# Moving 96 + 336 + 468 float32r matmuls to a fixed distance of 192 bytes between their two operands, and four small accumulations from ScalarE to VectorE

## The chip, the core and the metric

The kernel runs on one core of a Trainium2 chip. The metric is device time in microseconds; each number is the median of several runs of the whole program. A core has TensorE for matrix products (the profile's PE, with the weight loads shown beside it as PEld), VectorE (DVE), ScalarE (ACT), GpSimd (POOL, used here to issue DMAs) and SyncE (SP, which issues most loads). On-chip memory has 128 partitions, and a tile occupies the same bytes of each. "Distance" below always means the start address of a matmul's moving operand minus that of its stationary operand within a partition, modulo 256 bytes.

## What is computed

Two layers over 512 tokens of width 1024, with 256 context tokens that only the first layer needs:

```python
for i in range(DEPTH):                      # DEPTH = 2
    shift, scale, gate = split(silu(c) @ ada_w[i] + ada_b[i], 3)
    hx = rmsnorm(x, norm_g[i]) * (1 + scale) + shift          # hc: the same for the context
    if i == 0: out = retention_mixer(hx, hc, ...)             # 4 heads, both directions
    if i == 1: out = gmlp_chunk_mixer(hx, ...)                # v, u, z projections, spatial mix, output
    x = x + gate * out
return rmsnorm(x, final_g)
```

Retention projects q, k, v, z for each head, scores the 512 latent tokens against 768 keys with a decay, multiplies with v, normalises, gates with silu(z) and projects out. The gMLP projects v (2048 wide), normalises it over its width, mixes it over 128 tokens, multiplies with u and silu(z), and projects back to 1024.

## The kernel before, in words

All large products run in float32r with both operands split into a high and a low part; `mm3` (line of `mm3` in the listing) issues three matmuls for one product of two 128-row blocks: low x high, high x low, high x high. Each matmul record in the profile has one weight load (LDWEIGHTS) before it. A product of two 2x2-block matrices is done with seven block products (B11, T1, T2, B21, T3, B22, T4) by the class `Product`; one block product is 24 matmuls with 256 moving columns: 4 blocks of the contraction, 2 output halves, 3 matmuls.

Three functions carry these products. In `features` and `outward` the activations (tiles `A[...]`, in slots `oA11` to `oS4`, and `hc`) are moving and the weights stationary. In `tokens` it is the other way round. The weights come by DMA into raw slots (`w0` to `w7`, `g0`, ...), and `Stream.upto` splits them two products ahead into one of four `hl` slots, ScalarE making the high part and VectorE the low one. `hl_tile(moves)` starts the tile 128 bytes later in the slot or not, by whether the weights move. `place_at` instead puts the first four weight tiles of the gMLP's v projection straight into `oS1`, `oS2`, `oA22`, `oS3` (tile name `hl_e`).

The stages in order of time: the first projection with the start of the context (to 56 us); eleven more quads of weights, the projections of all heads (to 327); `attend_two`, heads 0 and 1 (to 380); `out_two`, their output projection (to 419); `attend_one` and `project_out` for heads 2 and 3 (to 522); the v projection of the gMLP (to 600); then eight units u0 to u7 of its u and z projection. After u3 comes `out_pair` (685 to 725), the first quarter products of the output projection, with `y` tiles split by `halved_y` into two separate slots each and weights (`o2`) moving. After u6 and after u7 follows `out1`, the rest of the output projection: weights (`o`) moving, 512 columns wide, `y` tiles stationary in `hc` (`ya`), in two `g` slots (`yb`) and in `oA11` (`yc`). In `attend`, `v` moves 512 wide and the score tiles `ph`, `pl` (slots `t2`) are stationary, 12 such matmuls a step, 288 in all; `out1` has 180 of them.

Each unit uses one tile `vt` (slot `w7`), loaded by `load_vt` on SP's queue and scaled by `norm_vt` with four ScalarE instructions; `spatial` multiplies it during B22. Before `out_pair`, `w7` is also lent to the raw loads of `o2` (`Q.free.append("w7")`), and `load_vt(4)` follows in the text after `out_pair`. The instructions of SP need not be in the order of the text: the framework places them.

`between_modes` is a small plain float32 matmul of `ones` (two records in the trace) that the text puts between groups of products at chosen places.

Slots are laid out by `lay` in the order of its lists, so addresses follow from sizes (each rounded up to 32 bytes). Modulo 256, counted from `oA11`:

| slots | before | after |
|---|---|---|
| activations in `oA*`, `oS*`; `hc`, `s1`, `w4`, `w5`, `g3` | 0 | 0 |
| `s0`, `s2`, `s3`, `rope`, `w6`, `g2`, `w0`-`w3`, `w7`, `g0`, `g1` | 64 | 64 |
| `t2` (score tiles `ph`, `pl`) | 192 | 64 |
| weights in `hl`, stationary / moving | 64 / 192 | 64 / 192 |
| weights in `hl` for `o` (512 wide in `out1`) | 64 | 192, or 0 for j = 9, 11 |
| weights in `hl` for `o2` (`out_pair`) | 192 | 0 |
| weights in `oS1`, `oS2`, `oA22`, `oS3` (`hl_e`) | 0 | 192 |

and so, moving minus stationary:

| matmuls | before | after |
|---|---|---|
| activations with `hl` weights in either role, score products of `qk` (about 5,500, 256 wide) | 192 | 192 |
| `hl_e` weights with `oA11`, `oA12` (96, 256 wide) | 0 | 192 |
| `o2` weights with `y` in `out_pair` (336, 256 wide) | 128 (272), 192 (64) | 192 |
| `v` with `ph`, `pl` (288, 512 wide) | 64 | 192 |
| `o` weights with `ya`, `yb`, `yc` in `out1` (180, 512 wide or split in two at the end) | 64, or 0 for half of `yb` | 192 |

Of the kernel before, what the change touches and what calls it, by code (L numbers as in the profile page):

```python
# [8 lines left out]
F32R = mybir.dt.float32r  # L9
# [58 lines left out]
def hybrid_kernel(ctx, tc, xT_d, cT_d, cv_d, sv_d, rows_d, ada0_d, adag_d, w_d, rope_d, dec_d, ws_d, id_d, out_d):  # L68
# [14 lines left out]
        return sb.tile(shape, dt, tag=tag, name=name or tag, bufs=bufs)  # L83

    T2 = 11
    HL = 4

    def lay(sizes, bufs=1):  # L90
        for tag, n in sizes.items():
            st([P, n // 4], tag, name="lay", bufs=bufs)

    lay({"ones": 512, "sv": 448, "ident": 512, "eps": 4, "cpad": 1024, "root": 4, "lg": 32, "gs0": 64, "sh0": 64,
         "sq0": 16, "sq1": 16, "sq2": 16, "rs0": 1024, "rs1": 1024, "rs2": 1024, "shb": 16, "gate0": 32, "gs1": 32,
         "sh1": 32, "shs": 16, "la": 32, "lb": 32, "lc": 32, "sum0": 16, "sum1": 16, "bns": 256, "mv": 32, "rv": 16})
# [58 lines left out]
    class Stream:  # L155
# [54 lines left out]
        def upto(self, n, late=None):  # L210

            while self.done < min(n, self.limit or len(self.items)):
                q, name, uses, at, place = self.items[self.done]
                self.pump()
                r = self.raws[q, at]
                self.sum(self.done)
                if self.by_queue(q, name):
                    if (q, name) not in self.added:
                        self.add((q, name))
                    assert (q, name) in self.added  # L220
                hl = place() if place else hl_tile(q[0] in ("vz", "v", "z", "v1", "o2"))
# [141 lines left out]
    for i in range(UZ):  # L363
        Q.quad(("u", i), SINGLE)
        for u in RAWS:
            Q.load((("u", i), u), W, 3, parts_of(("u", i), u))
        if i == 3:
            for name in PAIRED:
                for q in OUT1:
                    Q.item(q, name)  # L370
            for u in ("11", "21", "12", "22"):
                for q in OUT1:
                    Q.load((q, u), W + ["w7"], 3, parts_of(q, u))
        if i == UZ - 2:
            add_out(2, range(2))
    add_out(2, (2, 3))
# [3 lines left out]
    A = {}  # L380

    def op(key):
        A[key] = st([P, 2, 4, HS], "o" + key, F32R)

    def keep(key, src, ks=(0, 4)):
        k = slice(*ks)
# [375 lines left out]
    def come(*what, then=None):  # L762


        made = []
        for kb, th in what:
            g, k = divmod(kb, 4)
            r = th // 2
            if r:
                f, h, l = cq[g][:, k, :], hc[:, 0, kb, :], hc[:, 1, kb, :]  # L770
            else:
                name = NAMES[th][g]
                if k == 0:
                    A[name] = st([P, 2, 4, HS], AT_S3.get(name, "o" + name), F32R)
# [387 lines left out]
    def v_tile(h, tag):  # L1162

        if h != 1:
            return st([P, 2, 2, 512], tag, F32R, name="v")
        i = hls[0] % HL
        hls[0] += 1
        o = 16 if i % 2 else 48
        t = st([P, 2048 + o], f"hl{i}", F32R, name="v")
        return t[:, o:].rearrange("p (a b n) -> p a b n", a=2, b=2)  # L1170

    def load_v(h):
        v = []
# [169 lines left out]

    def attend_one(h, qs, vs, wo, steps, own=()):

        og = [st([P, 2, 4, HS], tag, F32R, name="og") for tag in ("oS3", "oS4")]

        def turn(h, hf, flipped):
            for fp, src in enumerate(flipped):
# [10 lines left out]
    def attend_two(qs, vs, ds, q2):  # L1360
# [2 lines left out]
        at = {}  # L1363

        def operand(key):
            t = A[key] = st([P, 2, 4, HS], ROOM[key], F32R)
            return t

        def plain(key, tag):
# [364 lines left out]
    def y_sums():  # L1734
        v = st([P, 4, HS], "g0", name="yv")
        dve.tensor_tensor(v, y22, y21, ALU.subtract)
        halved_y("S1", v, "g2", "g3")
        yield
        dve.tensor_tensor(v, v, y11, ALU.add)
        yield  # L1740
# [3 lines left out]
        dve.scalar_tensor_tensor(l, v, -1.0, f32(h), ALU.mult, ALU.subtract)  # L1744
        yield
        dve.tensor_tensor(y12, v, y12, ALU.subtract)
        halved_y("S4", y12, "g2", "g3")
        yield
        dve.tensor_tensor(y21, y11, y21, ALU.subtract)
        halved_y("S3", y21, "g0", "g1")  # L1750
        yield
        halved_y("A22", y22, "g2", "g3")
        yield

    def out_pair():
# [3 lines left out]
        for name in PAIRED:  # L1759
            for q in OUT1:  # L1760
# [137 lines left out]
    for i in range(UZ):  # L1898
        got, pms = {}, {}
        prod = Product(features, got.__setitem__)  # L1900
        for name in SINGLE:
# [11 lines left out]
            if name == "B22":  # L1913
# [135 lines left out]
```

## Time and profile before

| | |
|---|---|
| median of 3 runs | 863.49 us (861.56 to 864.96) |
| the profiled execution | 861.68 us, with a span of 859.8 us from first to last instruction |
| granted TensorE clock, mean | 0.998 |
| TensorE matmul / weight load busy | 850.1 / 821.2 us |
| VectorE / ScalarE / GpSimd busy | 723.8 / 487.8 / 88.9 us |
| TensorE waiting by name | 1.1 us at the start, 0.9 us for a `pl` tile, 0.8 us for `ident` |

Matmul records overlap, because their ends include the way through the array. What one matmul costs is therefore read from starts: in the timeline, the start of a row, subtracted from the start of the next row, divided by the row's count, is the spacing of those matmuls.

### The profile page before, as it was taken

How to read it: one execution, taken by the hardware profiler on the slowest of the kernel's cores; microseconds unless marked ns; L12 is line 12 of the kernel's file. 1: busy time of each engine (PE TensorE's matmuls, PEld its weight loads, DVE VectorE, ACT ScalarE, POOL GpSimd, SP SyncE). 2: the span in 40 equal slices, each digit the busy share in tenths (PEclk: the TensorE clock that was granted, in tenths of full speed). 3: DMA queues.
4: the chain of work that ended last, by engine and by line, in shares of the span. 5: the costliest groups of instructions: out<-in, count | busy, mean ns of one | idle time of the engine just before them, and what ended most of it. 6: DMA issues, size and time to landing. Idle time of an engine off the chain costs nothing.

```text
span 859.8 us, 17428 instructions
## 1 busy us (share of the span) xinstructions
PE 850.1 (99%) x6966; PEld 821.2 (96%) x6966; DVE 723.8 (84%) x1015; ACT 487.8 (57%) x770; POOL 88.9 (10%) x132
## 2 busy tenths in 40 slices
PE   9999999999999999999999999999999999999996
PEld 7899999999999999899989899999999999999985
DVE  4799899869977985799687879998888998788895
ACT  4566644455365355567873559754656665565434
POOL 0001211211211011000001012121000010000110
PEclk9999999999999999999999999999999999999999
DMA  9945857876977797257486943547555557546532
GB/s 358 406 131 154 245 175 255 261 216 183 311 218 226 221 305 264 75 123 219 162 273 186 261 113 111 197 135 244 173 148 144 152 129 215 154 141 197 123 49 99
DMA packets 82049, 166.70 MB, mean 194 GB/s; under 512 B 8624, under 2 KB 39728, under 8 KB 81968
## 3 DMA queue, kind: packets, MB, share of 16 engines
q1 hardware_dynamic: 68592, 122.90, 43.4%
q0 software_dynamic: 12944, 42.48, 20.1%
q8 instruction: 55, 0.90, 0.4%
q10 hardware_dynamic: 432, 0.20, 0.1%
q14 instruction: 26, 0.21, 0.1%
HBM read 125.17 MB, written 24.12 MB: 174 GB/s over the span
## 4 chain that ended last, share of the span: by engine, by line
PE 94%; ACT 3%; DMA 1%; DVE 1%; issue 1%; ACTq 0%; DVEq 0%
PE pst L54 94%; DMA vt<-vt 1%; DMA ident<-in_id_dram 1%; ACT acc L54 0%; DVE o L54 0%; ACT L54 0%; ACT junk L54 0%; ACT hl L54 0%; ACT dt L54 0%; ACT vt L54 0%; ACT qk L54 0%; DVE snap L54 0%; ACT de L54 0%; DVE ada_h L54 0%; DVE v L54 0%
## 5 line engine op out<-in xcount | busy, mean ns | idle before, releaser
L54 DVE TENSOR_TENSOR hl<-raw,hl 128x1024 fp32r<-128x1024 f32 (+2 forms) x209 | 249.7, 1200 | 56.4 <-ACT hl L54 55.9
L54 ACT CAST hl<-raw 128x1024 fp32r<-128x1024 f32 (+2 forms) x209 | 214.4, 1031 | 128.6 <-DVE raw L54 61.9
L54 PE MATMUL pst<-oS,hl 128*128 128x256 f32 x1296 | 155.2, 277 | 0.1
L54 PEld LDWEIGHTS pst<-oS,hl 128*128 128x128 f32 x1296 | 150.6, 188 | 1.2 <-issue 0.8
L54 PE MATMUL pst<-hl,oS 128*128 128x256 f32 x1152 | 134.7, 276 | 0.0
L54 PE MATMUL pst<-oA,hl 128*128 128x256 f32 x1080 | 133.9, 279 | 0.1
L54 PEld LDWEIGHTS pst<-hl,oS 128*128 128x128 f32 x1152 | 132.4, 188 | 0.8 <-issue 0.4
L54 PEld LDWEIGHTS pst<-oA,hl 128*128 128x128 f32 x1080 | 127.3, 188 | 1.8 <-issue 0.4
L54 DVE TENSOR_TENSOR raw<-raw 128x1024 f32<-128x1024 f32 x77 | 93.9, 1220 | 0.9
L54 PE MATMUL pst<-hl,oA 128*128 128x256 f32 x768 | 92.1, 277 | 0.0
L54 ACT ACTIVATE snap<-pst 128x512 f32<-128x512 f32 x87 | 51.7, 594 | 68.0 <-PE pst L54 67.9
L54 PEld LDWEIGHTS pst<-hl,oA 128*128 128x128 f32 x768 | 89.3, 188 | 0.0
L54 PE MATMUL pst<-v,ph 128*128 128x512 f32 x192 | 59.8, 393 | 0.0
L187 POOL DMA_DIRECT2D raw<-raw x31 | 27.0, 870 | 278.8 <-DVE raw L54 166.9
L54 DVE TENSOR_TENSOR snap<-snap,pst 128x512 f32<-128x512 f32 x75 | 51.0, 680 | 3.0 <-PE pst L54 2.9
L54 PE MATMUL pst<-og,hl 128*128 128x256 f32 x384 | 46.3, 280 | 0.0
L54 PEld LDWEIGHTS pst<-og,hl 128*128 128x128 f32 x384 | 45.0, 188 | 0.2
L54 PEld LDWEIGHTS pst<-v,ph 128*128 128x128 f32 x192 | 36.1, 188 | 7.0
L54 PE MATMUL pst<-hl,ye 128*128 128x256 f32 x336 | 40.4, 282 | 0.0
L54 PEld LDWEIGHTS pst<-hl,ye 128*128 128x128 f32 x336 | 40.1, 188 | 0.1
L54 PE MATMUL pst<-v,pl 128*128 128x512 f32 x96 | 37.8, 394 | 0.9 <-DVE pl L54 0.9
L54 ACT CAST ph<-pf 128x512 fp32r<-128x512 f32 x24 | 14.9, 621 | 40.2 <-DVE pf L54 40.2
(240 smaller groups left out, 1134.9 us busy)
## 6 DMA issues: line engine op xcount, KB each, us to landing
raw<-in_w_dram SPq DMA_DIRECT2D x208, 256.0 KB, 3.9
bg<-in_adag_dram SPq DMA_DIRECT2D x32, 512.0 KB, 5.1
raw<-raw POOLq DMA_DIRECT2D x31, 512.0 KB, 5.4
ada_w<-in_ada_dram SPq DMA_DIRECT2D x16, 512.0 KB, 8.5
raw<-in_w_dram SPq DMA_DIRECT2D x16, 512.0 KB, 4.5
v<-snap POOLq DMA_DIRECT2D x16, 256.0 KB, 4.6
z<-snap POOLq DMA_DIRECT2D x16, 256.0 KB, 4.5
v<-v SPq DMA_DIRECT2D x8, 512.0 KB, 6.7
```

What stands on the lines that cost most here:

```text
L54: made = op(*args, **kw)
L187: nc.gpsimd.dma_start(self.raws[q, to], self.raws[q, src], accum_op=ALU.add)
```

## The change

The slots are reordered and the tiles shifted within their slots as in the tables above. `oA22`, `oS1`, `oS2` and `oS3` become 64 bytes larger and their activations start 64 bytes in, while raw tiles and `hl_e` start at the slot's beginning; small tiles fill the space between so that each of these slots starts at the same residue. The four `hl` slots get one size, and `hl_part` computes the shift from the wanted residue. `out_pair`'s low parts move from `g3` to `w7` (A11's from `s1` to `g1`), so that all its `y` tiles lie at 64; `g3` instead of `w7` is lent to the raw loads of `o2`. In `out_two`, the block row "21" (two products, two instructions each) is accumulated into `acc` on VectorE.

```diff
-    HL = 4
+    HL, HL_SIZE = 4, 8384
+    def big(shape, tag, name=None):
+        o = AHEAD // 4 if tag in ("oA22", "oS1", "oS2", "oS3") else 0
+        t = st([P, 2048 + o], tag, F32R, name=name)[:, o:]
+        return t.rearrange("p (a b c) -> p a b c", a=shape[1], b=shape[2])
...
-    lay({"oA11": 8192, "oA12": 8192, "oA22": 8192, "oS1": 8192, "oS2": 8192, "oS3": 8192, "oS4": 8192, "hc": 16384,
-         "s1": 4096, "w4": 4096, "w5": 4096, "g3": 4096, "cv": 64})
-    lay({"s0": 4096, "s2": 4096, "s3": 4096, "rope": 4096, "w6": 4096, "g2": 4096, "hl0": 8576})
+    AHEAD = 64
+    lay({"oA22": 8192 + AHEAD, "sv": 448, "oS1": 8192 + AHEAD, "lg": 32, "gs0": 64, "sh0": 64, "gate0": 32, "oS2": 8192 + AHEAD,
+         "gs1": 32, "sh1": 32, "la": 32, "lb": 32, "lc": 32, "mv": 32, "oS3": 8192 + AHEAD})
+    lay({"oA11": 8192, "oA12": 8192, "oS4": 8192, "hc": 16384, "s1": 4096, "w4": 4096, "w5": 4096, "g3": 4096, "cv": 64})
+    lay({"s0": 4096, "s2": 4096, "s3": 4096, "rope": 4096, "w6": 4096, "g2": 4096})
     lay({"t2": 2048}, T2)
-    lay({"hl1": 8320, "hl2": 8576, "hl3": 8320})
+    lay({f"hl{i}": HL_SIZE for i in range(HL)})
...
-    def hl_tile(moves=False):
+    STATIONARY, MOVING, SHIFTED = 0, 128, -64
+    def hl_part(to, name):
         i = hls[0] % HL
         hls[0] += 1
-        t = st([P, 2080], f"hl{i}", F32R, name="hl")
-        o = 32 if moves != (i % 2 == 1) else 0
-        return t[:, o:o + 2048].rearrange("p (a n) -> p a n", a=2)
+        t = st([P, HL_SIZE // 4], f"hl{i}", F32R, name=name)
+        o = (to - i * HL_SIZE) % 256 // 4
+        return t[:, o:o + 2048]
...
+        def home(self, q):
+            if q[0] == "o2" or (q[0] == "o" and q[1] in (9, 11)):
+                return SHIFTED
+            return MOVING if q[0] in ("vz", "v", "z", "v1", "o") else STATIONARY
...
-                    Q.load((q, u), W + ["w7"], 3, parts_of(q, u))
+                    Q.load((q, u), W + ["g3"], 3, parts_of(q, u))
...
-                    act.activation(acc[:, m, th * HS:th * HS + HS], t[:, s * HS:s * HS + HS], AF.Copy, scale=gate0[:, m:m + 1])
+                    to, src, g = acc[:, m, th * HS:th * HS + HS], t[:, s * HS:s * HS + HS], gate0[:, m:m + 1]
+                    if name == "21":
+                        dve.tensor_scalar(to, src, g, None, ALU.mult)
+                    else:
+                        act.activation(to, src, AF.Copy, scale=g)
...
-        halved_y("S1", v, "g2", "g3")
+        halved_y("S1", v, "g2", "w7")
...
-        halved_y("S4", y12, "g2", "g3")
+        halved_y("S4", y12, "g2", "w7")
...
-        halved_y("A22", y22, "g2", "g3")
+        halved_y("A22", y22, "g2", "w7")
...
+        Q.free.remove("g3")
         gb = Q.gate = st([P, D], "g1", name="gb")
-        late_rows["fg"] = fg = st([P, D], "g0", name="fg")
+        late_rows["fg"] = fg = st([P, D], "g3", name="fg")
-        ys.extend([ya[:, i] for i in range(4)] + [st([P, 2, SEQ], f"g{i}", F32R, name="yb") for i in (2, 3)])
+        ys.extend([ya[:, i] for i in range(4)] + [st([P, 2, SEQ], tag, F32R, name="yb") for tag in ("g0", "g2")])
...
                 if i == 3:
-                    Q.free.append("w7")
+                    Q.free.append("g3")
...
-                halved_y("A11", y11, "s0", "s1")
+                halved_y("A11", y11, "s0", "g1")
...
             out_pair()
-            Q.free.remove("w7")
             load_vt(4)
```

Everywhere else the diff only takes `big` or `hl_part` in place of the plain allocation.

More of the change, by code (lines that the diff above doesn't have):

```diff
@@ L92, in lay, with hl_tile @@
             st([P, n // 4], tag, name="lay", bufs=bufs)
-    lay({"ones": 512, "sv": 448, "ident": 512, "eps": 4, "cpad": 1024, "root": 4, "lg": 32, "gs0": 64, "sh0": 64,
-         "sq0": 16, "sq1": 16, "sq2": 16, "rs0": 1024, "rs1": 1024, "rs2": 1024, "shb": 16, "gate0": 32, "gs1": 32,
-         "sh1": 32, "shs": 16, "la": 32, "lb": 32, "lc": 32, "sum0": 16, "sum1": 16, "bns": 256, "mv": 32, "rv": 16})
+    lay({"ones": 512, "ident": 512, "eps": 4, "cpad": 1024, "root": 4, "sq0": 16, "sq1": 16, "sq2": 16, "rs0": 1024, "rs1": 1024,
+         "rs2": 1024, "shb": 16, "shs": 16, "sum0": 16, "sum1": 16, "bns": 256, "rv": 16})
     lay({"ada_s": 16, "ss": 8}, 2)
     lay({"fss": 8}, 4)
-    lay({"oA11": 8192, "oA12": 8192, "oA22": 8192, "oS1": 8192, "oS2": 8192, "oS3": 8192, "oS4": 8192, "hc": 16384,
-         "s1": 4096, "w4": 4096, "w5": 4096, "g3": 4096, "cv": 64})
-    lay({"s0": 4096, "s2": 4096, "s3": 4096, "rope": 4096, "w6": 4096, "g2": 4096, "hl0": 8576})
+    AHEAD = 64
[3 more added lines that the diff above has]
+    lay({"s0": 4096, "s2": 4096, "s3": 4096, "rope": 4096, "w6": 4096, "g2": 4096})
     lay({"t2": 2048}, T2)
-    lay({"hl1": 8320, "hl2": 8576, "hl3": 8320})
+    lay({f"hl{i}": HL_SIZE for i in range(HL)})
     lay({"w0": 4096, "w1": 4096, "w2": 4096, "w3": 4096, "w7": 4096, "g0": 4096, "g1": 4096, "dec": 4 * TW})
     hls = [0]
-    def hl_tile(moves=False):
+    STATIONARY, MOVING, SHIFTED = 0, 128, -64
+    def hl_part(to, name):
         i = hls[0] % HL
         hls[0] += 1
-        t = st([P, 2080], f"hl{i}", F32R, name="hl")
-        o = 32 if moves != (i % 2 == 1) else 0
-        return t[:, o:o + 2048].rearrange("p (a n) -> p a n", a=2)
+        t = st([P, HL_SIZE // 4], f"hl{i}", F32R, name=name)
+        o = (to - i * HL_SIZE) % 256 // 4
+        return t[:, o:o + 2048]
+    def hl_tile(to=STATIONARY):
+        return hl_part(to, "hl").rearrange("p (a n) -> p a n", a=2)
     def t2(name, shape=(P, 512), dt=F32):
@@ L220, in upto @@
                     assert (q, name) in self.added
-                hl = place() if place else hl_tile(q[0] in ("vz", "v", "z", "v1", "o2"))
+                hl = place() if place else hl_tile(self.home(q))
                 split((hl[:, 0, :], hl[:, 1, :]), r, late)
@@ L382, in op @@
     def op(key):
-        A[key] = st([P, 2, 4, HS], "o" + key, F32R)
+        A[key] = big([P, 2, 4, HS], "o" + key)
     def keep(key, src, ks=(0, 4)):
@@ L773, in come @@
                 if k == 0:
-                    A[name] = st([P, 2, 4, HS], AT_S3.get(name, "o" + name), F32R)
+                    A[name] = big([P, 2, 4, HS], AT_S3.get(name, "o" + name))
                 f, h, l = xk(th, g, k), A[name][:, 0, k, :], A[name][:, 1, k, :]
@@ L1164, in v_tile @@
         if h != 1:
[L1165 to L1170, printed above, removed]
+            return big([P, 2, 2, 512], tag, "v")
+        return hl_part(SHIFTED, "v").rearrange("p (a b n) -> p a b n", a=2, b=2)
     def load_v(h):
@@ L1344, in attend_one @@
     def attend_one(h, qs, vs, wo, steps, own=()):
-        og = [st([P, 2, 4, HS], tag, F32R, name="og") for tag in ("oS3", "oS4")]
+        og = [big([P, 2, 4, HS], tag, "og") for tag in ("oS3", "oS4")]
         def turn(h, hf, flipped):
@@ L1365, in operand @@
         def operand(key):
-            t = A[key] = st([P, 2, 4, HS], ROOM[key], F32R)
+            t = A[key] = big([P, 2, 4, HS], ROOM[key])
             return t
```

## The prediction

> **What bounds the kernel now.** I read the page first: busy times, then the chain that ended last. Then the timeline of TensorE by stage, to turn starts into spacings, and last the timelines of ScalarE, VectorE and the SP queue at the two places where the change moves work.
>
> ```profile
> span 859.8 us, 17428 instructions
> PE 850.1 (99%) x6966; PEld 821.2 (96%) x6966; DVE 723.8 (84%) x1015; ACT 487.8 (57%) x770; POOL 88.9 (10%) x132
> PE 94%; ACT 3%; DMA 1%; DVE 1%; issue 1%; ACTq 0%; DVEq 0%
> ```
>
> TensorE is busy for 99% of the span and carries 94% of the chain. So the time is 6966 times the spacing of one matmul, plus a few stalls, and a change of addresses can act only on the spacing. This is the timeline of TensorE in a quiet stage, the v projection of the gMLP and the start of u0:
>
> ```profile
> 573.28 21.92 PE L54 MATMUL pst<-hl,oS 128*128 128x256 f32 x192
> 595.04 5.61 PE L54 MATMUL pst<-hl,oA 128*128 128x256 f32 x48
> 600.48 2.28 PE L54 MATMUL pst<-oA,hl 128*128 128x256 f32 x18
> 602.60 0.39 PE L54 MATMUL pst<-ones 128*128 128x128 f32 x2
> ```
>
> 192 matmuls in 595.04 - 573.28 = 21.76 us are 113.3 ns each. All are at distance 192 already, as are some 5,500 in all (the table of addresses). But the next row, also at 192, has 18 in 2.12 us: 117.8 ns. Distance 192 thus has two speeds, a fast one at 113.3 and a slow one 4.5 ns longer. Here the slow one begins where the roles change: weights move before 600.48 and stand after it, so the last moving tile (192) and the first new stationary one (64) are 128 apart for one overlap. It can last for long:
>
> ```profile
> 674.98 5.11 PE L54 MATMUL pst<-oS,hl 128*128 128x256 f32 x42
> 679.93 1.05 PE L54 MATMUL pst<-wsT,vt 128*128 128x128 f32 x8
> ```
>
> 42 in 4.95 us are 117.9 ns, again at 192, up to the next float32 matmuls. So the change does not speed up most of the kernel; it can act on the 900 matmuls that are elsewhere, and on which of the two speeds the others are in.
>
> **Part 1, `out_pair`, 336 matmuls, 272 of them at 128.**
>
> ```profile
> 685.24 3.71 PE L54 MATMUL pst<-hl,ye 128*128 128x256 f32 x30
> 688.79 0.38 PE L54 MATMUL pst<-ones 128*128 128x128 f32 x2
> 688.93 36.71 PE L54 MATMUL pst<-hl,ye 128*128 128x256 f32 x306
> 725.47 1.76 PE L54 MATMUL pst<-oA,hl 128*128 128x256 f32 x14
> ```
>
> The stage takes 725.47 - 685.24 = 40.23 us, of which the two `ones` are 0.14: 119.3 ns each. At 192 it takes 336 x 113.3 ns = 38.07, and the first 30, after a change of roles and before `ones`, 4.5 ns more: 0.13. With 0.14 for `ones` 38.34, a saving of 1.9 us. If it were slow throughout, 336 x 117.8 = 39.58, it saves 0.5.
>
> **Part 2, `hl_e`, 96 matmuls at 0.**
>
> ```profile
> 521.81 3.04 PE L54 MATMUL pst<-hl_e,oA 128*128 128x256 f32 x24
> 524.69 1.03 PE L54 MATMUL pst<-ident,acc 128*128 128x128 f32 x8
> ```
>
> 24 in 2.88 us are 120.0 ns. At 113.3 the 96 save 0.64 us; the first 24 follow a change of roles, and I take them as slow (0.11 back): 0.5. Slow throughout it is 0.2.
>
> These two parts rest on distance alone being the cause. The Trainium skill speaks against that: "TensorE: Matmul & The Clock Gate", Part 2, step 1, says that TensorE has two independent SBUF read ports and that loading the next weights takes no read bandwidth from the running matmul. By that rule the order of slots would not change the spacing, parts 1 to 4 would be nothing, and only part 5 would be left. The trace disagrees, with 113.3, 119.3 and 120.0 ns for matmuls of one shape; it is a rival below.
>
> **Part 3, 468 matmuls of 512 columns, from 64 (some 24 from 0) to 192.** No such matmul stands at 192 without a wait before, so this is bounded. In `out1` and in the attention:
>
> ```profile
> 833.88 1.54 PE L54 MATMUL pst<-hl,ya 128*128 128x512 f32 x6
> ...
> 848.99 1.54 PE L54 MATMUL pst<-hl,yc 128*128 128x512 f32 x6
> 850.36 0.84 PE L54 MATMUL pst<-hl,ya 128*128 128x256 f32 x6
> 851.04 0.84 PE L54 MATMUL pst<-hl,yc 128*128 128x256 f32 x6
> ```
>
> ```profile
> 331.35 0.39 PE L54 MATMUL pst<-v,pl 128*128 128x512 f32 x1
> ...
> 334.11 1.58 PE L54 MATMUL pst<-qk 128*128 128x256 f32 x12
> ```
>
> From 833.88 to 848.99 are 11 rows of 6: 15.11 us over 66 are 228.9 ns; the 12 of an attention step are 2.76 us, 230. The last rows are the same tiles at 64 with 256 columns: 6 in 0.68 us, 113.3. So 64 costs nothing at 256 columns and, at 512, 2.3 to 3.3 ns more than twice 113.3 (226.7). If 192 is as good at 512 as its fast speed at 256, it saves 2.3 x 468 = 1.1 us; at its slow speed (226.7 + 4.5 = 231.2) it costs 2.3 x 468 = 1.1 us. Both kinds of row exist; the fast one is by far the more common at 192, so I weight it four to one: -0.65 us, with both ends kept.
>
> **Part 4, the speeds that products inherit.** After `out_pair` u4 changes roles. It does so today too, but coming from the mixed distances of `ye`, and it is fast:
>
> ```profile
> 728.20 5.60 PE L54 MATMUL pst<-oS,hl 128*128 128x256 f32 x48
> 733.64 2.88 PE L54 MATMUL pst<-oA,hl 128*128 128x256 f32 x24
> ```
>
> 48 in 5.44 us, 113.3. After the change it comes from a clean stretch at 192, as the slow row at 600.48 did, and no `ones` follows; the next float32 matmuls are those of `spatial`, after 5 x 24 + 18 = 138 matmuls. I take it as slow: 138 x 4.5 = +0.6 us. u7 after `out1` changes roles as well; its overlap goes from 0 to 128. I take half of the same: +0.3. Ends for both together: 0 and +1.2.
>
> **Part 5, the four accumulations.** They matter at one place, the start of head 2, the 0.91 us for which TensorE waits:
>
> ```profile
> 420.23 0.82 ACT L54 ACTIVATE acc<-pst,gate 128x256 f32<-128x256 f32 x2
> 420.43 0.69 DVE L54 SCALAR_TENSOR_TENSOR pf<-pst,dt 128x512 f32<-128x512 f32 x1 [0.98 <-PE pst L54]
> 420.94 1.05 ACT L54 CAST v<-v 128x1024 fp32r<-128x1024 f32 x1
> 421.88 0.85 ACT L54 ACTIVATE acc<-pst,gate 128x256 f32<-128x256 f32 x2
> 422.60 0.64 ACT L54 CAST ph<-pf 128x512 fp32r<-128x512 f32 x1
> 423.27 0.69 DVE L54 TENSOR_TENSOR pl<-pf,ph 128x512 fp32r<-128x512 f32 x1
> 424.02 0.50 PE L54 MATMUL pst<-v,pl 128*128 128x512 f32 x1 [0.91 <-DVE pl L54]
> ```
>
> On ScalarE `ph` stands behind the `v` cast and both pairs of accumulations, which end 0.7 us (420.94 - 420.23) and 0.7 us (422.60 - 421.88) later than without them. Without them the `v` cast ends near 421.3 and `ph` waits for `pf`. VectorE gets four instructions:
>
> ```profile
> L54 DVE TENSOR_TENSOR o<-snap,pst 128x256 f32<-128x256 f32 x12 | 4.6, 415 | 0.1
> ```
>
> By this nearest row, also from PSUM, they are 4 x 0.415 = 1.7 us at most, 0.98 of it in the idle time that the row of `pf` shows, so `pf` is up to 0.7 us late: ends at 421.8. `ph` then ends at 422.4, VectorE's low part of `v` (1.2 us) by 423.0, and `pl` starts between 422.5 and 423.0 in place of 423.27. That is 0.3 to 0.8 us earlier; I take -0.6, with 0.9 (the whole stall) and 0 as ends. The accumulations' results are needed only at 445 us.
>
> **Part 6, `w7`.** After the change `w7` holds a low part of `y` until the last matmul of `out_pair`, so `load_vt(4)` cannot start before 725.5.
>
> ```profile
> 708.90 0.33 SPq L54 DMA_DIRECT2D vt<-vt  x1
> 710.04 9.47 SPq L54 DMA_DIRECT2D raw<-in_w_dram  x8
> 719.66 0.33 SPq L54 DMA_DIRECT2D gb<-gate  x1
> 730.62 6.84 SPq L54 DMA_DIRECT2D raw<-in_w_dram  x8
> ```
>
> Today it goes at 708.90. In the text it stands behind `gb`, so SP's order is the framework's, by expected readiness, and I expect it to be put where SP is idle, between 720 and 730. Its scaling on ScalarE, then about 731 to 733, is due at 739 for `spatial`. What such a late `vt` can cost is shown in u2, in the chain:
>
> ```profile
> 640.01 5.60 DMA vt<-vt
> 646.14 1.57 ACT vt L54 x3
> 647.72 0.49 ACT snap L54
> 648.25 199.54 PE pst L54 x1562
> ```
>
> There the copy that frees a product's bank stood behind the scaling, and TensorE started T2 about 0.25 us late. I take +0.25. If u4 has the same order on ScalarE, landing at 731 delays T2, due at 730.9, to 733.4: +2.5; the other end is 0.
>
> **The sum.** -1.9 - 0.5 - 0.65 + 0.9 - 0.6 + 0.25 = -2.5 us. The profiled execution is 861.68 us (span 859.8 and 1.9 around it), 1.8 us below the median of 863.49, so the same difference is put on the median: 861.0 us, 0.3% less. About 0.5%, 4.3 us, is what a measurement of this kernel can tell from no change.
>
> **The rivals.**
>
> *All at the fast speed.* Every product at 192 stays at 113.3, 512 columns come at 226.7, and the stall goes: -2.0 - 0.64 - 1.1 - 0.9 = -4.6 us, 858.9. For it: 192 matmuls in a row without one slow. Against: the slow rows at 600.48 and 674.98. Chance 0.25, for a saving over 0.5%.
>
> *The ports are independent and addresses do nothing.* The 119.3 and 120.0 ns would then come from those stages' other traffic. Only part 5 and 6 remain: -0.35 us, 863.1. Against it: one shape in the same kind of stage goes at 120.0 ns at 521.81 and at 113.3 some 50 us later. Chance 0.06.
>
> *512 columns slow, and u4's copy behind the scaling.* -1.9 - 0.5 + 1.1 + 1.2 - 0.6 + 2.5 = +1.8 us, 865.3, slower than before by less than 0.5%. Chance 0.06.
>
> *The load of `vt` heads SP's queue.* If the framework leaves it at its place of today, the 8 raw loads at 710.04, which are u4's weights, wait behind it until 726. The first then lands some 3 us later, its split takes 2.3 us (1.05 on ScalarE, 1.2 on VectorE), and the first product, due at 725.5, starts at 731.7; the next three raw tiles come 2.4 us apart (9.47 us for 8) and cost about one more: +7.2 us, with the rest +4.7, 868.2. It decides as soon as any load needed before 733 stands behind `vt`. Against it: SP's order is by readiness. Chance 0.06.
>
> **How the numbers follow.** The forecast, between -4.3 and -0.5 us, has 0.57. Faster by over 0.5%: the first rival and a part of the forecast's edge, 0.27. Slower by over 0.5%: the last rival, 0.06. Within: 0.67. The range runs from 858.0, the fast case with 0.1% for the measurement, to 864.8, which takes in the second rival and most of the third; the last is left out.
>
> **What would show it.** In the profile after, the `hl,ye` matmuls should be 38.3 us for 336 and `hl_e` 2.7 to 2.8 us for 24; the rows of 512 columns should be 1.36 us for 6 if fast, 1.39 if slow (1.37 now); u4's first products should be 117.8 ns if part 4 is right; the `pl` wait at 420 should be 0.1 to 0.6 us; and `vt` should be issued near 725.5 with u4's raw loads before it. The prediction is wrong if `ye` or `hl_e` keep 119 to 120 ns, or if TensorE waits in u4.

## The result and the profile after

The change makes the kernel slower. After it the median is 867.87 us (865.35 to 870.66, 11 runs), and the kernel before gave 863.11 us beside it (861.56 to 864.96, 11 runs): a ratio of 1.0059, 95% interval 1.0044 to 1.0075. The forecast was 861.0 us with a range of 858.0 to 864.8, so the sign was wrong and the range missed. The profiled execution took 868.1 us (span 865.9), against 861.68 (859.8) before. These two lie 6.4 us apart, the medians 4.8: one pair of profiles shows more than the typical loss.

Below, the speed of a matmul is its spacing, start to start, as in the prediction: **fast** is 113.3 ns for 256 columns, **slow** 117.8.

From the page of the kernel after:

```profile
PE 854.3 (99%) x6966; PEld 822.6 (95%) x6966; DVE 725.8 (84%) x1019; ACT 485.9 (56%) x766; POOL 89.1 (10%) x132
PE 88%; DMA 4%; DVE 3%; ACT 2%; issue 1%; SPq 0%; DVEq 0%; ACTq 0%
```

TensorE's share of the chain fell from 94% to 88%, and VectorE's rose from 1% to 3%: there is a new bound somewhere. Both kernels issue the same 6966 matmuls in the same order, so the start of one matmul can be set against the start of the same one. That gives where the 6.2 us came from (second column: a second execution of the unchanged kernel after, told of below):

| stretch (times of the kernel before) | forecast, us | after, us | again, us |
|---|---|---|---|
| to 250 | 0 | 0.0 | 0.0 |
| 250 to 331, two stretches that begin behind `columns` | 0 | +1.6 | +1.6 |
| 331 to 419 and 426 to 495, attention and its output | -0.4 (part 3) | +1.2 | +1.2 |
| 419 to 426, start of head 2 | -0.6 (part 5) | +0.6 | +0.6 |
| 495 to 541, with `hl_e` | -0.5 (part 2) | -0.3 | +0.1 |
| 541 to 648 | 0 | +0.1 | +0.1 |
| 648 to 685, u2 and u3 | 0 | +0.6 | -0.4 |
| 685 to 725, `out_pair` | -1.9 (part 1) | -0.3 | -0.4 |
| 725 to 790, u4 to u6 | +0.6 (part 4), +0.25 (part 6) | +2.1 | 0.0 |
| 790 to the end, `out1` and u7 | -0.25 (part 3), +0.3 (part 4) | +0.6 | +0.6 |

Now the rows that answer to those of the prediction. TensorE's timeline from `out_pair` to u4:

```profile
689.09 3.70 PE L54 MATMUL pst<-hl,ye 128*128 128x256 f32 x30
692.62 0.39 PE L54 MATMUL pst<-ones 128*128 128x128 f32 x2
692.76 16.14 PE L54 MATMUL pst<-hl,ye 128*128 128x256 f32 x139
709.22 19.94 PE L54 MATMUL pst<-hl,ye 128*128 128x256 f32 x167 [0.31 <-DVE hl L54]
728.99 2.99 PE L54 MATMUL pst<-oA,hl 128*128 128x256 f32 x24
731.82 5.82 PE L54 MATMUL pst<-oS,hl 128*128 128x256 f32 x48
737.47 2.99 PE L54 MATMUL pst<-oA,hl 128*128 128x256 f32 x24
```

`out_pair` takes 728.99 - 689.09 = 39.9 us, not 38.3. Most of the 139 matmuls behind `ones` come at 113.3 ns; then comes a wait for VectorE's `hl`, and behind it the last 167 are slow, as are u4's: 24 in 2.83 us and 48 in 5.65 us, 117.8 ns. The chain of the same kernel shows who sets the pace in `out_pair`, where before it was TensorE alone from 648.25 for 199.54 us:

```profile
651.51 37.76 PE pst L54 x320
...
696.40 1.22 DVE yv L54
697.62 1.14 DVE hl L54
699.09 1.13 DVE ye L54
...
709.22 144.68 PE pst L54 x1071
```

`hl_e` (timeline of TensorE): the first 24 come in 2.74 us, 114 ns in place of 120, but the 30 behind them end in a wait for `sums`: 0.46 us from start to start, where the slower matmuls before the change had 0.14.

```profile
525.08 2.90 PE L54 MATMUL pst<-hl_e,oA 128*128 128x256 f32 x24
527.82 1.04 PE L54 MATMUL pst<-ident,acc 128*128 128x128 f32 x8
528.61 3.66 PE L54 MATMUL pst<-hl_e,oA 128*128 128x256 f32 x30
532.45 0.68 PE L54 MATMUL pst<-ident,sums 128*128 128x128 f32 x4 [0.18 <-DVE sums L54]
```

512 columns in `out1` (timeline of TensorE, first and last of thirteen such rows): 13 x 6 in 856.52 - 838.32 = 18.20 us are 233.3 ns, where 64 had 228.9.

```profile
838.32 1.56 PE L54 MATMUL pst<-hl,yc 128*128 128x512 f32 x6
...
855.12 1.56 PE L54 MATMUL pst<-hl,yc 128*128 128x512 f32 x6
856.52 0.85 PE L54 MATMUL pst<-hl,ya 128*128 128x256 f32 x6
```

The start of head 2, all engines:

```profile
421.56 0.87 DVE L54 TENSOR_SCALAR acc<-pst,gate 128x256 f32<-128x256 f32 x2
...
422.44 1.04 ACT L54 CAST v<-v 128x1024 fp32r<-128x1024 f32 x1
423.51 1.22 DVE L54 TENSOR_TENSOR v<-v 128x1024 fp32r<-128x1024 f32 x1 [1.07 <-ACT v L54]
424.65 0.68 DVE L54 SCALAR_TENSOR_TENSOR pf<-pst,dt 128x512 f32<-128x512 f32 x1
...
425.39 1.30 PE L54 MATMUL pst<-qk 128*128 128x256 f32 x9 [1.43 <-DVE pf L54]
```

`pf` no longer stands ahead of `v` on VectorE but behind it, and TensorE waits 1.43 us for `pf` where it waited 0.91 for `pl`. And a place that the prediction leaves out, the transposes of `columns` at 250 us and what follows them:

```profile
250.02 0.38 PE L54 MATMUL pst<-ident,cole 128*128 128x128 f32 x2
250.23 0.39 PE L54 MATMUL pst<-ones 128*128 128x128 f32 x2
250.38 5.90 PE L54 MATMUL pst<-hl,oA 128*128 128x256 f32 x48
256.12 5.82 PE L54 MATMUL pst<-hl,oS 128*128 128x256 f32 x48
261.77 2.99 PE L54 MATMUL pst<-hl,oA 128*128 128x256 f32 x24
```

48 in 261.77 - 256.12 = 5.65 us: slow, at distance 192, up to the role change at 273. Before, the same matmuls took 113.3.

### The profile page after: what moved, and what is told of

It reads as the page before. It is cut to its first block, busy times and chain, and to the rows that moved or that the text cites. A ratio compares the mean times of both kernels' runs of the same rounds, so it can differ in the third digit from the quotient of the medians.

```text
span 865.9 us, 17424 instructions
## 1 busy us (share of the span) xinstructions
PE 854.3 (99%) x6966; PEld 822.6 (95%) x6966; DVE 725.8 (84%) x1019; ACT 485.9 (56%) x766; POOL 89.1 (10%) x132
## 4 chain that ended last, share of the span: by engine, by line
PE 88%; DMA 4%; DVE 3%; ACT 2%; issue 1%; SPq 0%; DVEq 0%; ACTq 0%
PE pst L54 88%; DMA ada_w<-in_ada_dram 1%; DMA raw<-in_w_dram 1%; DMA cq<-in_cT_dram 1%; DMA xs<-in_xT_dram 1%; DVE hl L54 1%; DMA vt<-vt 1%; DVE o L54 0%; DVE ye L54 0%; DVE raw L54 0%; ACT L54 0%; DVE yv L54 0%; DVE yq L54 0%; ACT acc L54 0%; ACT junk L54 0%
## 5 line engine op out<-in xcount | busy, mean ns | idle before, releaser
L54 PE MATMUL pst<-hl,ye 128*128 128x256 f32 x336 | 39.8, 280 | 0.3 <-DVE hl L54 0.3
```

Source lines behind the costliest of these rows:

```text
L54: made = op(*args, **kw)
```

## The experiments

Three theories at the start. **A**: a distance of 192 has two speeds, a stretch keeps the one with which it begins, what runs just ahead of it sets that, and 512 columns are slower at 192 than at 64. **B**: speed goes by distance alone, and the loss is waits. **C**: it is chance, the speed is drawn anew in each execution. A1 to A3 are what might set it; D and E came up for `out_pair`.

**Spacing by distance, alone.** A kernel of nothing but matmuls, 48 (256 columns) or 24 (512) at each distance, three times with other work ahead, and changes of role at 192.

> This kernel leaves the whole computation out. It runs products of 48 float32r matmuls of 256 columns, and of 24 of 512, at each distance from 0 to 224 bytes in steps of 32, each time behind one plain float32 matmul, behind two, and behind a wait for VectorE; at the end it changes the roles of two tiles six times at distance 192. If distance 192 has two speeds (theory A), the spacing at 192 and 256 columns is 113.3 ns behind some of these and 117.8 behind others, and a speed lasts to the next interruption; at 512 columns 192 is then 226.7 or about 232, not better than the 229 of distance 64. If the spacing is a function of the distance alone (rival B), every stretch at one distance has one spacing, and 192 has 113.3 and 226.7.

Steady spacing, ns, worked out from the starts of the single matmuls:

| distance | 0 | 32 | 64 | 96 | 128 | 160 | 192 | 224 |
|---|---|---|---|---|---|---|---|---|
| 256 columns | 120.0 | 116.4-117.8 | 117.8 | 120.0 | 118.4-120.0 | 117.4-118.9 | 117.8 or 113.3 | 118.3 |
| 512 columns | 226.7-228.1 | 233.3 | 228.9 | 233.3 | 231.9-232.8 | 234.3 | 233.3 | 233.3 |

So 192, the only distance with 113.3 ns for 256 columns in this run, is one of the worst for 512. (It is not the only one in the kernel: the last rows before, at 64, came at 113.3 as well, as the prediction shows at 850.36.) All three products at 192 in the first part were slow, two of them behind pairs of `ones`; 113.3 came only in the second part, where the roles change. At its two role orders the new weights are loaded either 0 or 128 bytes from the last moving tile. After 128 the next stretch was slow in 4 of 4; after 0 a slow stretch became fast in 4 of 4, and a fast one slow in 2 of 2.

**Both kernels again, one execution each.**

> The changed kernel once more, for a second profile. Theory A with a speed that is set by addresses and order: the same stretches are slow as in the first profile (206 matmuls after 250 us, 213 after 307, all of u4 to u6), about 1,900 slow matmuls at distance 192. Rival C, chance: the slow stretches lie elsewhere and their number differs by several hundred.

> The kernel before once more, for a second profile. Theory A: about 675 slow matmuls at distance 192, in the same stretches as in the first profile (around 320 to 346, 501 to 521, 669 to 685 us). Rival C: their number comes near to that of the changed kernel.

The kernel after took 865.17 us (span 863.0). Its stretches at 250, 307, 381 and 448 us were slow as before, its 512 columns took 233.0 ns (before, twice: 229.5), and its wait at head 2 was there. But u3 and u4 to u6 were fast this time. TensorE's timeline at u4:

```profile
709.12 19.22 PE L54 MATMUL pst<-hl,ye 128*128 128x256 f32 x167 [0.33 <-DVE hl L54]
728.17 2.88 PE L54 MATMUL pst<-oA,hl 128*128 128x256 f32 x24
730.89 5.60 PE L54 MATMUL pst<-oS,hl 128*128 128x256 f32 x48
736.33 2.88 PE L54 MATMUL pst<-oA,hl 128*128 128x256 f32 x24
```

72 in 736.33 - 728.17 = 8.16 us, 113.3. So C holds for a part (648 to 685 and u4 to u6, 3.1 us between the two executions), and not for the rest. u4 takes on the speed with which `out_pair` ends: of the five profiles with this seam and no pair of `ones` at it, both were slow here and there (this kernel's first, and the one with `ident` moved, below) or both fast (this one, 512 columns at 64, `cole` moved). The kernel before again took 861.52 us. It was not the same all through either: the stretch at 669 us was fast this time, 0.4 us less to 685 us, and `out_pair` behind it took 40.9 us in place of 40.2, with a wait for VectorE's `ye` (41.0 in the run of the accumulations alone, below).

**A pair of `ones` ahead of u4**, in the kernel after.

```diff
-            if (i, name) == (0, "B11"):
+            if (i, name) in ((0, "B11"), (4, "B11")):
```

> The changed kernel with one more small float32 matmul of ones, in the third quarter of u4's first product. Theory A: u4 to u6 take the fast speed, some 450 matmuls by 4.5 ns, 2.0 us less than the changed kernel, 1.0037 of the kernel before. Rival B (the loss is stalls and 512 columns): 0.1 us more than the changed kernel, 1.006. Rival C: no difference that can be told.

865.63 us, ratio 1.0033 (1.0021 to 1.0044), near A's number. u4 to u6 were fast in the profile, and the pair costs 0.24 us. But `out_pair` had ended fast in this profile already, so it does not show that the pair did it. The runs that show it come below: where `out_pair` ended slow (512 columns at 0, and the sums left out), u4's first 18 matmuls came at 117.8 ns, and behind the pair it was 113.3.

**512 columns at 64 again**, in the kernel after (`t2` laid between `hl1` and `hl2`; the second part of the edit, not shown, starts `o` 128 bytes further on):

```diff
+    lay({f"hl{i}": HL_SIZE for i in range(2)})
     lay({"t2": 2048}, T2)
-    lay({f"hl{i}": HL_SIZE for i in range(HL)})
+    lay({f"hl{i}": HL_SIZE for i in range(2, HL)})
```

> The kernel after, but every 512-column product is laid 64 bytes apart again, as before the change (the attention's `v` and `out1`'s weights and moving tiles); all else stays. Theory A (speed goes by distance and width, 192 is the slow distance for 512 columns, 64 a better one): the 512-column mean goes from 233.0 back to about 229.5 ns, 462 x 3.5 ns = -1.6 us, and the slow 256-column stretches that are entered from a 512-column product at 381 and 448 us (36 and 48 matmuls) go: -0.4 us; so 2.0 us less than after, a ratio to before of about 1.0035 where after had 1.0059. Theory B (address distance does nothing to 512 columns; the loss is stalls): the ratio stays at 1.006 and the mean at 233.

863.6 us, ratio 1.0010 (0.9996 to 1.0025): 4 us less, twice what A promised. The 512-column mean went to 230.0 ns and the slow stretches at 381 and 448 went, as A has it. But those at 250 and 307 went too: `cole` lies in a `t2` slot, and so I had moved it as well.

**`ident` moved**, so that the two `cole` transposes are 128 apart as before.

```diff
-    lay({"ones": 512, "ident": 512, "eps": 4, "cpad": 1024, "root": 4, ...
+    lay({"ones": 512, "eps": 4, "root": 4, "ident": 512, "cpad": 1024, ...
```

> The kernel after, with only the slot of `ident` moved, so that the transposes of `cole` against `ident` at 250 and 307 us are 128 bytes apart as before the change (64 in the kernel after). Theory A1 (which of its two speeds a stretch at 192 takes is set by the distances of the few matmuls just ahead of it, here the two transposes): the stretches of some 207 and 215 slow matmuls behind 250 and 307 us come back to 113.3 ns, 422 x 4.5 ns = -1.9 us, ratio about 1.0037. Theory A2 (what sets it is not the distance of the transposes but what stands after them or the time at which they come): the two stretches stay at 117.8 ns, ratio about 1.006. Theory C (the speed is drawn anew in each execution): one or the other, differing between the two stretches.

The ratio, 1.0037 (1.0024 to 1.0051), is A1's number, and A1 is wrong all the same. The timeline of TensorE shows the stretch as slow as ever:

```profile
256.58 5.82 PE L54 MATMUL pst<-hl,oS 128*128 128x256 f32 x48
262.23 2.99 PE L54 MATMUL pst<-hl,oA 128*128 128x256 f32 x24
```

The ratio moved for some other reason; the stretches of chance are one that would do, but no run shows it. The same caution holds for the other ratios against that of the kernel after. Only the stretch itself could decide. With the addresses of all these kernels side by side one number was left: from the last moving tile ahead of the transposes (192) to `cole` it is 128 bytes where the stretch is slow, and 0 (or 192, in one kernel below) where it is fast.

**`cole` moved, and nothing else**, in the kernel after.

```diff
-        e = t2("cole", (P, HS))
+        e = t2("cole", (P, 512))[:, 32:32 + HS]
```

> The kernel after, with one slot moved: `cole`, which the transposes ahead of 250 and 307 us load as weights, lies 128 bytes further, so that the last moving tile before it (192) and `cole` are 0 apart as before the change, not 128; `ident` and all else stay. Theory A3 (a stretch takes the slow speed where the weights loaded under the last product ahead of the interruption lie 128 bytes from its moving tile): the stretches of 207 and 215 matmuls behind 250 and 307 us go at 113.3 ns, -1.9 us, ratio to before about 1.0037 where after had 1.0059, if the chance stretches behind 650 us fall as they did. Theory A2 (something else sets them): the two stretches stay at 117.8 ns, ratio about 1.006.

864.97 us, ratio 1.0030 (1.0016 to 1.0044). Both stretches are fast; the first in TensorE's timeline, 48 in 5.44 us:

```profile
256.33 5.60 PE L54 MATMUL pst<-hl,oS 128*128 128x256 f32 x48
261.77 2.88 PE L54 MATMUL pst<-hl,oA 128*128 128x256 f32 x24
```

One tile of 1 KB a partition, used in two transposes of 0.1 us, decides over 420 matmuls and 1.6 us behind them. A3 stands at this place. (The move also put the transposes themselves 192 apart in place of 64; that this is not the cause is shown by the combined kernel below, which has them 128 apart, like the kernel with `ident` moved, and whose matmuls here come at 113.3 ns.) As a rule A3 has gaps. The last moving tile lay at 192 in every one of these kernels, so its distance to `cole` and `cole`'s own address cannot be told apart. In the isolated run an overlap of 0 turned a fast stretch slow, where here it stays fast. And in the kernel before u4 also loads its weights (64) 128 bytes from `out_pair`'s last moving tile (192), and was fast in all three profiles (728.20 in the prediction).

**The four accumulations alone**, in the kernel before.

> The kernel before, with the four accumulations on VectorE and nothing else. My prediction's part 5 expected TensorE's wait of 0.91 us at 424 us to shrink by 0.6. Theory A (the framework puts two accumulations and the low part of `v` ahead of `pf` on VectorE, so that `pf` comes later than before): one gap of about 1.7 us in the qk scores in place of the gap of 1.19 us ahead of the first product of `v`; +0.5 us. Theory B (the later `pf` in the kernel after came of its addresses or its slower matmuls): the gap is 0.3 to 0.6 us.

All engines at head 2, with 1.43 us of waiting for `pf`:

```profile
418.76 0.87 DVE L54 TENSOR_SCALAR acc<-pst,gate 128x256 f32<-128x256 f32 x2
...
421.83 0.68 DVE L54 SCALAR_TENSOR_TENSOR pf<-pst,dt 128x512 f32<-128x512 f32 x1
...
422.57 0.62 PE L54 MATMUL pst<-qk 128*128 128x256 f32 x3 [1.43 <-DVE pf L54]
```

The stretch from 419 to 426 us is 0.53 us longer than before, as in the kernel after (0.56). It is the accumulations by themselves. The run's time was 863.0 us; this one also had a wait of 0.8 us for a `snap` at 818 us that has nothing to do with them.

**All repairs together**: accumulations on ScalarE again, `ones` ahead of u4, 512 columns at 64 or at 0, `cole` clear of 128.

> The kernel after with four repairs: the four accumulations back on ScalarE, 512-column products at 64, `ident` moved so that the `cole` transposes are at 128, and one pair of `ones` matmuls ahead of u4. Theory A: -1.65 (512 columns), -0.4 (slow 256 behind them), -1.9 (250 and 307 us), -1.9 (u4 to u6, from the run with the pair of `ones`), -0.5 (wait at head 2) from 867.9 give 861.5, a ratio of 0.998 (0.996 to 1.000): what is left of the change is then `out_pair` and `hl_e`, -2.0 and -0.56 us. Theory B (the loss is stalls only): about 1.005.

> As the combined kernel at 64, but the 512-column products at distance 0 in place of 64 and `ident` left in the place that the change gives it (`cole` transposes then at 128 with this lay). Theory A, with the steady spacing of the micro run (512 columns: 226.7 ns at 0, 228.9 at 64, 233.3 at 192): another -1.0 us against the combined kernel at 64 if the 462 matmuls come in steady runs, ratio about 0.997; the mean of 512 columns 227 to 228. Where they come in short runs between 256-column products (the attention), the micro run shows 228.1 at first: -0.6 us. Theory B: the same time as the combined kernel at 64.

At 64 it took 862.43 us, ratio 0.9986 (0.9977 to 0.9995): faster than the kernel before by 0.14%, about what `out_pair` brings. That is a small margin: the medians of the kernel before, measured beside the different runs, range from 862.27 to 863.55 us. At 0 it took 862.71, ratio 0.9994 (0.9985 to 1.0004), not the 0.997 expected: the 512 columns went only from 229.7 to 228.7 ns. In `out1` the rows with `ya` and `yc` came at the expected 226.7, but those where `ya` and `yb` alternate at some 230, and in the attention, in short runs, the mean was 228.6; behind these runs 11 or 12 of 12 score products were slow in every step.

**Why `out_pair` gives so little.** In the combined kernel it took 39.2 us at an average of 113.9 ns outside the waits. Three sums of `y` were moved from VectorE to GpSimd, or left out.

```diff
-        dve.tensor_tensor(v, v, y11, ALU.add)
+        nc.gpsimd.tensor_tensor(v, v, y11, ALU.add)
...
```

> The combined kernel at 64, with three sums of `y` in `out_pair` (128x1024, 1.22 us each on VectorE) on GpSimd. Theory D (in `out_pair` VectorE, busy 100% from 685 to 707 us in the profiles, sets the pace as soon as the matmuls come at 113.3 ns, so that most of part 1's gain is given back as waits of TensorE for `ye` and `hl`): without them VectorE has 3.7 us less in that stretch, the gaps of some 600 to 900 ns at 698 and 707 us go, and `out_pair` takes 38.3 to 38.6 us in place of 39.2 to 39.8; 0.6 us less than the combined kernel, ratio to before about 0.998, unless GpSimd is so slow that TensorE waits for its sums (a gap of over 1 us in the same place). Theory E (the gaps are weights that come late from memory): they stay, 39.2 to 39.8 us.

> The combined kernel at 64, with the same three sums of `y` left out (the rest of the reference is computed with `y11`, `y12`, `y21`, `y22` and the first difference in their place). Theory D: as with the sums on GpSimd but without a wait for it, `out_pair` takes 38.2 to 38.5 us if its matmuls are in the fast speed (39.7 if they are slow), with no gap over 300 ns. Theory E: gaps of 600 to 900 ns stay and it takes 39.2 to 39.8 us.

On GpSimd the kernel lost 10.7 us (873.42, ratio 1.0124, 1.0105 to 1.0142): a sum takes 2.4 to 3.2 us there, VectorE's splits beside the first two took 3.07 and 3.29 us in place of 1.22, and TensorE waited 2.5 and 4.8 us for `ye`. Behind the waits some matmuls came 213 ns apart; the granted clock was 0.66 from 707 to 717 us, where the combined kernel has 1.00. Left out (862.39 us), the wait near 706 us went and the one near 697 stayed, as TensorE's timeline shows:

```profile
688.45 7.74 PE L54 MATMUL pst<-hl,ye 128*128 128x256 f32 x66
696.81 28.51 PE L54 MATMUL pst<-hl,ye 128*128 128x256 f32 x240 [0.62 <-DVE ye L54]
725.15 0.52 PE L54 MATMUL pst<-oA,hl 128*128 128x256 f32 x3
```

That is half of D: the sums lie behind the first wait on VectorE and could not shorten it. The 240 were slow in this run, so `out_pair` took 40.2 us. (With slow matmuls ahead, the wait near 706 us is only 0.2 us in the other profiles too.) So the difference ahead of that wait was put behind its split, which then splits `y22` instead:

```diff
-        dve.tensor_tensor(v, y22, y21, ALU.subtract)
-        halved_y("S1", v, "g2", "w7")
+        halved_y("S1", y22, "g2", "w7")
+        dve.tensor_tensor(v, y22, y21, ALU.subtract)
```

> The combined kernel at 64, but the split of `S1` in `out_pair` takes `y22` in place of the difference `y22 - y21`, which is made behind it (the rest of the reference is computed with this wrong `S1`). The `ye` that TensorE waits for near 697 us then no longer stands behind that difference (1.22 us) on VectorE. Theory D (VectorE's queue sets the pace there): the gap of 880 to 900 ns at 697 us shrinks to under 250 ns, in a run where the matmuls ahead of it are fast; VectorE's later work is the same, so a gap may come later in its place, at the weights' low parts near 700 us. Theory E (the wait is for data from memory or for ScalarE): the gap stays at 880 to 900 ns.

```profile
690.30 16.03 PE L54 MATMUL pst<-hl,ye 128*128 128x256 f32 x139
707.04 19.20 PE L54 MATMUL pst<-hl,ye 128*128 128x256 f32 x167 [0.72 <-DVE hl L54]
```

The first wait is gone, and a longer one (0.72 in place of some 0.3 us) stands at the next weights' low part. The first half says little: the 30 matmuls ahead came at 117.8 ns here, and behind matmuls at that speed there was no such wait in the kernel after and in the combined kernel either. What speaks for D and against E is VectorE itself: without these edits it has no idle time from 685 to 711 us, before or after the change, so it is not held up by data from memory or by ScalarE there, and TensorE's waits are for what it makes. Shorten its queue at one point and TensorE waits at the next.

**`ones` ahead of u7 as well**, in the combined kernel.

> The combined kernel at 64 with a second pair of `ones` matmuls, ahead of u7. In the combined kernel u7 ran slow (158 matmuls at 117.8 ns from 799 us, 0.7 us) in the one profile. Theory A (a pair of `ones` takes a stretch that carries the slow speed back to the fast one, as ahead of u4): -0.7 us for the speed and +0.24 us for the pair, the ratio to before falls from 0.9986 to about 0.998. Theory C (the speed is drawn anew in each execution and `ones` has no hold on it): u7 may stay slow, and the ratio is 0.9986 to 0.999.

u7's first 18 matmuls, ahead of the pair, were slow in the profile, and all behind it fast, as A expected:

```profile
798.64 2.28 PE L54 MATMUL pst<-oA,hl 128*128 128x256 f32 x18
800.75 0.38 PE L54 MATMUL pst<-ones 128*128 128x128 f32 x2
800.89 0.94 PE L54 MATMUL pst<-oA,hl 128*128 128x256 f32 x6
801.67 5.60 PE L54 MATMUL pst<-oS,hl 128*128 128x256 f32 x48
807.11 2.88 PE L54 MATMUL pst<-oA,hl 128*128 128x256 f32 x24
```

18 in 2.11 us are 117.2 ns, 48 in 5.44 are 113.3. The slow start is a product of the repair: with 512 columns at 64, the last `o` tile ahead of u7 and u7's weights are 64 apart, and u7 was slow in all six profiles with that (here as far as the pair), and in none of the others. The time, 862.5 us, ratio 0.9989 (0.9976 to 1.0002), is the same as without it within the interval; the half microsecond was not to be seen.

## Why the prediction was wrong, point by point

*What bounds the kernel.* TensorE's 99% and the idea that addresses act on the spacing held. The Trainium skill's rule of two independent read ports ("TensorE: Matmul & The Clock Gate", Part 2, step 1), read as in the prediction, that the order of slots would not change the spacing, does not agree with the runs: 113.3 to 120.0 ns for 256 columns and 226.7 to 234.3 for 512, by the distance and by what ran before. That the ports are where it happens is not shown.

*Part 1, `out_pair`: mis-sized, -0.3 in place of -1.9 us (-1.1 at best, with the repairs).* The matmuls can come at the speed forecast: in the second execution all of them did, 113.4 ns, and the stage still took 39.8 us, because two waits for VectorE, near 699 and 709 us, add 1.5 us from start to start. (In the first execution the last 167 were slow instead.) The step costed the matmuls as if nothing else were near its limit. The profile of before says otherwise in its busy time by engine for this stage (columns: PE, PEld, DVE, ACT, POOL busy, then granted clock, DMA share, GB/s):

```profile
685.00:707.00 22.00, 22.00 (x187) 21.92 (x186) 22.00 (x27) 14.89 (x18) 2.53 (x3) 1.00 0.51 110
```

VectorE is busy for 22.00 of 22 us. In the second execution of the kernel before, and in the run of the accumulations alone, where a fast u3 brought TensorE to this stage sooner, it waited there for VectorE already. The 84% on the page is an average over the kernel; here there was nothing left to go faster with.

*Part 2, `hl_e`: right in the matmuls* (120.0 to 114.0 ns over the 96, -0.57 us), most of it given back to the wait for `sums` and the seam behind: from 522 to 541 us 0.1 us is left. The rest of the -0.3 in the table lies ahead of `hl_e`, where fewer matmuls were slow in that execution.

*Part 3, 512 columns: wrong, +1.6 in place of -0.65 us.* The mean went from 229.5 to 233.0 ns, 462 x 3.5 ns. The step set its ends by twice the 256-column speeds (226.7 and 231.2) and took the fast one four to one; no row of the profile had 512 columns at 192, and the truth lay outside both ends. Nor does 64 "cost nothing" at 256 columns: it has two speeds as well, 113.3 at 850.36 before, 117.8 in the isolated run and in the last rows of the kernel with 512 columns at 64 again.

*Part 4, inherited speeds: the step that failed most.* I held that a change of roles makes a stretch slow and that the next float32 matmuls end it. What the runs point to is the distance for the one overlap at the seam: the slow speed followed 128 at `cole` in each profile that had it there and at four role changes (105, 178, 272 and 600 us) in every profile, while 192 carried on what was at u4 in the five profiles told of above; u4 before, at 128 and fast, is the exception and stays open. After the change, `out_pair`'s last moving tile (0) and u4's weights (64) are 192 apart; my table of addresses said so, and I did not work out that overlap. `spatial`'s float32 matmuls carry the speed on as well, in every unit of the fifteen profiles: slow lasted to the end of u6, 2.1 us in place of 0.6 in one execution and 0 in the other. For u7 I took an overlap of 128; by the table it is 192 (the last `o` tile at 0, for j = 9), and u7 was fast, 0 in place of +0.3. The quoted stretch at 674.98 before in fact goes on behind the float32 matmuls at 679.93 (117.8 ns again from 682.65 on); I took them for its end. And I listed only role changes as seams, not the transposes of `columns` (+1.6 us) nor the steps from 512 to 256 columns.

*Part 5, the accumulations: wrong sign, +0.55 in place of -0.6 us.* I let `pf` wait behind two accumulations, at most 0.7 us. The framework also put the low part of `v` (1.22 us, behind 1.07 us of idling for ScalarE's cast of `v`) ahead of it. In part 6 I had reckoned with a placed order, and only on SP's queue.

*Part 6, `vt`: the load went where I said* (issued at 728.95 us, behind u4's raw loads), and its scaling at 733.45 cost TensorE nothing that the trace shows, in place of 0.25.

*The rivals.* The third (512 slow, u4 slow) named two of the causes and had 0.06. The last one's 868.2 us is next to the measured 867.87 by luck: it has TensorE wait for u4's weights behind `vt`, and that did not happen. The forecast needed the fast speed nearly everywhere; the chances counted it as the common one because most stretches before had it, without asking what had given it to them.

*Left open:* what in the chip sets the two speeds; what makes `out_pair` end slow or fast behind its waits; why u4 before is fast; why u2's wait at 651 us leads to the slow speed in some executions and not in others; the slow stretch that follows a gap of 0.25 us at 313 us in the kernel with 512 columns at 0.

## What to carry to other kernels

Before a faster operation is counted as time, take the busy time of every engine in that stage alone: the page's average hides an engine that is already full there. Where a spacing depends on addresses, list every seam between kinds of work, small transposes too, and work out the distances on both sides of each; a tile used for 0.2 us set the speed of the next 23 us here. And a ratio that matches a theory's number proves nothing until the stretch that the theory speaks of has been looked at.

## What the runs showed of the hardware that was not expected

- At distance 192, 256-column float32r matmuls with new weights each time come at 113.3 or at 117.8 ns, for hundreds in a row; small float32 matmuls between (`spatial`) carried the speed on each time, while a pair of `ones` inside a product at 192 was followed by 113.3 each time, also where it had been 117.8 (u0, u4, u7). `ones` is no reset everywhere: behind the transposes at 250 us after, and in the isolated run at 192 (143.45 us), 117.8 followed it.
- In the isolated run the best distance depends on the width: 192 for 256 columns (113.3 or 117.8, against 116.4 to 120.0 elsewhere), 0 and 64 for 512 (226.7 and 228.9 against 232 to 234). In the kernel 64 gave 113.3 for 256 columns too.
- A float32 sum of 128x1024 took 2.4 to 3.2 us on GpSimd and 1.22 on VectorE, and VectorE's own subtractions of that size beside it took 3.07 and 3.29 us.
